# Experts in a fixed order of whole quarters, the embedding's products during the choice of tokens, and the scan's arrays under the first weight buffers

## The chip, the cores and the metric

The kernel runs on one core of a Trainium2 chip. The metric is the device time of one execution in microseconds (us). The kernel before was timed three times: 1959.51, 1963.56 and 1964.66 us, so the median is 1963.56 us. Each time below comes from one profiled execution, and "at 503" means 503 us after the start of its span.

TensorE (PE) runs the matmuls, VectorE (DVE) and ScalarE (ACT) move results out of PSUM and do the small arithmetic, GpSimd (POOL) does some wide additions, and SyncE (SP) issues nearly all DMAs. SP does so strictly in the order of its program: a DMA whose buffer is not yet free holds up all that stand behind it.

## The reference, cut to what matters

Two layers, sequence 512, width 1024, float32. In each layer a mixer (a projection, three groups of sequence operations, among them a gated-delta scan, and an output projection) is followed by the part that the change is about:

```python
def expert_choice_ffn(h, w_router, w_gate, w_up, w_down):
    cap = EC_CAPACITY * S // N_EXPERTS            # 64 tokens for each of 16 experts
    aff = jax.nn.softmax(jnp.einsum('bsd,de->bse', h, w_router), axis=-1)
    gate, idx = lax.top_k(aff.transpose(0, 2, 1), cap)
    xe = jax.vmap(lambda hb, ib: hb[ib])(h, idx)  # gather
    hid = silu(einsum('becd,edf->becf', xe, w_gate)) * einsum('becd,edf->becf', xe, w_up)
    ye = einsum('becf,efd->becd', hid, w_down) * gate[..., None]
    y = zeros((B_ * S, D)).at[flat].add(ye.reshape(-1, D))   # scatter
...
x = x + expert_choice_ffn(rmsnorm(x, g_ffn[i]), ...)
e = rmsnorm(einsum('bsq,qd->bsd', p[i], w_ple[i]), g_ple[i])      # the embedding
x = x + e * sigmoid(rmsnorm(x, g_ple_gate[i]) @ w_ple_gate[i])
```

`w_gate`, `w_up` and `w_down` are 1024x1024 for each of 16 experts: 192 MB of float32 in a layer, and each byte is used once.

## The kernel before

**Pairs and gemms.** The experts run in eight pairs `pi`. An expert has 64 tokens, so two share the 128 output partitions: expert `ei` of a pair writes partitions 64*ei to 64*ei+63. For each pair `gemm` (L1268 to L1279) runs three times: gate into `pGt`, up into `pUp`, down into `pY`. One gemm is four quarters of the inner dimension. A quarter needs one weight tile from each of the two experts, 128x2048 float32 = 1,048,576 bytes, and issues 8 matmuls with `ei` innermost, so two neighbours write different halves of the columns. The trace has two records for each float32 matmul: 16 in a quarter, 64 in a gemm. A layer has 23 such gemms, that is 184 tiles. The 24th, the last pair's down product, is done in column quarters with 16 tiles `wd` of 512 KB (L1387, L1391); the gate of the embedding ends the layer.

**Other work on PE in this stage.** `gather` builds the tokens of two pairs at a time with matmuls `xep` against one-hot matrices (L1206, L1207), with the transposes `otp` and the small products `pgs` (L1220 to L1229). `scatter` multiplies back, `ysc` (L1295, L1296), and DVE adds it to `x` (L1301). Two groups of transposes `htp` (L1349) turn `hid` between up and down. After pair 5 `ple_e` multiplies the embedding, `plep` (L1172), and normalises it (`e`, L1181, L1182).

**The order.** For the first pair the four gate quarters and the first gather are interleaved by hand. All else is left to a scheduler which orders instructions by priority and readiness: a scatter's or gather's matmuls may go into the middle of a quarter.

**The weights.** `etile` (L1250 to L1265) takes the next buffer of the `ring` (L1241): five `wx`, three pairs of buffers of other names (used once), one `gslot`, then twelve `slot`. That is 21 tiles ahead at first. At the first scatter `taken(2)` gives two slots to the new `x`; after pair 5 two more go to `e` and three are moved back in the ring. Tiles stay with the buffer that the ring gives, and SP issues them in the program's order.

**The stages.** In the first layer the mixer goes to about 400 us, the router and the top-k (on DVE, eight rounds) to 446, the experts from 449 to 912 and the tail to about 985. The second layer has the same sequence; its first gate matmul starts 963 us later, at 1412.8. Buffers of the mixer lie where the expert stage's buffers come later; placeholders (`place`, L380 to L383) settle which mixer arrays lie under which.

Of the kernel before, what the change touches and what calls it, by code (L numbers as in the profile page):

```python
# [20 lines left out]
D = 1024  # L21
S = 512
# [95 lines left out]
class K:  # L118
# [938 lines left out]
    def moe(self, l):  # L1057
# [60 lines left out]

        wk = ep.tile([64, S // 2], F32, tag="OT", name="topk", bufs=3)
# [28 lines left out]
        pe.matmul(pr[:, 1], ones, rr_(above[:, 2, None, :]).to_broadcast([128, NT, NE]), start=False, stop=True)  # L1148
        rank = ep.tile([128, NT, NE], F32, name="rank")
# [3 lines left out]
        self.tap("rank", rank)  # L1153
        affr = ep.tile([128, NT, NE, 2], F32, name="affr")
        rsr = ep.tile([128, NT, 2], F32, name="rsr")

        def ple_e():

            self.mark("ple_e")
            gple = self.slot("gple")[:, :D]  # L1160
            self.row(gple, l, "g_ple")
            pTt = self.slot("pT")[:, :2 * S].rearrange("p (k n) -> p k n", k=2)
            nc.scalar.dma_start(pTt, A["pT"][l].rearrange("(k p) t -> p k t", p=128))
            wple = self.wtile(A["w_ple"][l], 1024, nk=2)
            self.ee = [self.slot("e").rearrange("p (t d) -> p t d", t=2) for _ in range(2)]
            es = ep.tile([128, NT, 2], F32, name="es")
            er = ep.tile([128, NT], F32, name="er")
            for t in range(NT):
                for half in range(2):
                    p = self.pb([128, 512], "plep")  # L1170
                    for k in range(2):
                        pe.matmul(p, pTt[:, k, t * 128:(t + 1) * 128], wple[:, k, half * 512:half * 512 + 512],  # L1172
                                  start=(k == 0), stop=(k == 1))
                    ev = e(t)[:, half * 512:half * 512 + 512]
                    act.activation(ev, p, AF.Square, accum_out=es[:, t, half:half + 1])
                    v.tensor_copy(ev, p)
# [7 lines left out]
        e = lambda t: self.ee[t // 2][:, t % 2, :]  # L1184
# [5 lines left out]
        def gather(qd):  # L1190
            self.mark("gather")
            OH = ep.tile([128, NT, 4, CAP], F32, tag="OH", name="OH", bufs=1)
            for t in range(NT):
                v.tensor_tensor(rr_(OH[:, t]), iota[:, None, :].to_broadcast([128, 4, CAP]),  # L1194
                                rank[:, t, 4 * qd:4 * qd + 4, None].to_broadcast([128, 4, CAP]), op=ALU.is_equal)
            OHf = rr_(OH.rearrange("p t e s -> p t (e s)"))
            xe = self.gslot("xe").rearrange("p (k n) -> p k n", k=KD)
            for pi in (0, 1):
                self.xe[2 * qd + pi] = xe[:, :, 128 * pi:128 * pi + 128]
            for kp in range(4):  # L1200
                self.mark("gather")
                for kk in (2 * kp, 2 * kp + 1):
                    p = self.pb([128, 4 * CAP], "xep")
                    ks = every(2, kk)
                    for t in range(NT):
                        pe.matmul(p, rr_(hh[:, t, ks]), OHf[:, t, :], start=(t == 0), stop=False)  # L1206
                        pe.matmul(p, rr_(hl[:, t, ks]), OHf[:, t, :], start=False, stop=(t == NT - 1))  # L1207
                    act.activation(xe[:, kk, :], p, AF.Copy, scale=gE[:, kk:kk + 1])
# [7 lines left out]
            for pi in (2 * qd, 2 * qd + 1):  # L1216
# [4 lines left out]
                OT = ep.tile([128, NT, 128], F32, tag="OT", name="OT", bufs=3)  # L1221
                act.activation(rr_(OT), p.bitcast(F32), AF.Copy)
                pgs = self.pc([128, 6], "pgs")
                for t in range(NT):
                    pe.matmul(pgs[:, 0:4], OHf[:, t, s0:s0 + 128],
                              rr_(affr[:, t, 2 * pi:2 * pi + 2, :].rearrange("p e s -> p (e s)")),
                              start=(t == 0), stop=(t == NT - 1))
                for t in range(NT):
                    pe.matmul(pgs[:, 4:6], OHf[:, t, s0:s0 + 128], rr_(rsr[:, t, :]),  # L1229
                              start=(t == 0), stop=(t == NT - 1))  # L1230

                gsl = ep.tile([128, 4], F32, tag="gsl", name="gsl", bufs=4)
                v.tensor_reduce(gsl[0:64, 0:1], pgs[0:64, 0:2], axis=AX.X, op=ALU.add)
                v.tensor_reduce(gsl[64:128, 0:1], pgs[64:128, 2:4], axis=AX.X, op=ALU.add)
                v.tensor_reduce(gsl[:, 3:4], pgs[:, 4:6], axis=AX.X, op=ALU.add)
                v.tensor_scalar(gsl[:, 1:2], gsl[:, 3:4], 0.5, None, op0=ALU.mult)
                v.tensor_tensor(gsl[:, 2:3], gsl[:, 1:2], gsl[:, 3:4], op=ALU.mult)
                self.OT[pi], self.gsl[pi] = OT, gsl
# [3 lines left out]
                     + ["slot"] * SLOTS)  # L1242
# [24 lines left out]
        def gemm(ws, lhs, pt):  # L1267

            for q in range(4):
                self.mark("experts")  # L1270
                wt = [etile(ws[ei][q * 256:(q + 1) * 256, :]) for ei in range(2)]
                for k in range(2):
                    kk = q * 2 + k
                    for nh in range(2):
                        for ei in range(2):
                            pe.matmul(pt[nh][64 * ei:64 * ei + 64, :], lhs[:, kk, 64 * ei:64 * ei + 64],  # L1276
                                      wt[ei][k][:, nh * 512:nh * 512 + 512],
                                      start=(kk == 0), stop=(kk == KD - 1))
                yield  # L1279

        def run(gen):
            for _ in gen:
                pass

        def scatter(pi, yh, yl):
# [5 lines left out]
            for t in range(NT):  # L1291
                for nh in range(2):
                    ns = slice(nh * 512, nh * 512 + 512)
                    p = self.pb([128, 512], "ysc")
# [5 lines left out]
                    else:  # L1300
                        v.tensor_tensor(xv, p, xv, op=ALU.add)  # L1301

        prev = None
        for pi in range(NE // 2):
            self.mark("experts")
            es_ = [2 * pi, 2 * pi + 1]
            if pi == 0:
                g0 = gather(0)
                piece = self.in_order()
                piece(g0)  # L1310
# [3 lines left out]
            if pi == 0:  # L1314

                for _ in range(4):
                    piece(gate)
                    piece(g0)
                run(g0)
            run(gate)  # L1320
# [3 lines left out]
            for nh in range(2):  # L1324
                sv = sg[:, nh * 512:nh * 512 + 512]
                act.activation(sv, pG[nh], AF.Tanh, scale=gsl[:, 1:2])  # L1326
                v.scalar_tensor_tensor(sv, sv, 1.0, pG[nh], op0=ALU.add, op1=ALU.mult)  # L1327
            pU = [self.pg([128, 512], "pUp") for _ in range(2)]
            run(gemm([A["w_e_up"][l, i] for i in es_], xe, pU))
# [14 lines left out]
            self.mark("experts")  # L1344
            for nh in range(2):
                p = self.pc([128, 4, 128], "htp")
                for k in range(4):
                    kk = nh * 4 + k
                    pe.transpose(p[:, k, :], hid[:, every(2 if pi < NE // 2 - 1 else 4, kk)], self.ident)  # L1349
                act.activation(hidT[:, nh * 4:nh * 4 + 4, :], p, AF.Copy)  # L1350
            if pi == NE // 2 - 1:
                break
            pY = [self.pg([128, 512], "pY") for _ in range(2)]
            run(gemm([A["w_e_down"][l, i] for i in es_], hidT, pY))
# [149 lines left out]
```

## Time and profile before

| | us |
|---|---|
| median of three runs | 1963.56 |
| the profiled execution | 1962.08 |
| its span (first to last instruction) | 1960.3 |
| PE busy in the span | 1809.5 |
| DVE / ACT / POOL busy | 931.7 / 523.9 / 457.4 |
| experts of layer 0 (window 449 to 909): PE busy, DMA share | 456.93, 0.94 |
| experts of layer 1 (window 1412 to 1885): PE busy, DMA share | 467.69, 0.93 |

Busy time is the union of an engine's instructions; a PE that is busy is not PE at its peak, since a matmul that runs alone occupies it as well as two that share it. "DMA share" is the mean busy share of the 16 DMA engines, and GB/s what they moved. In a timeline "x16" is a run of 16 records of one group, its first number the start and its second the time to the end of the last. "[10.25 <-DVE topk L1132]" is idle time just before, and what ended it.

### The profile page before, as it was taken

How to read it: one execution, taken by the hardware profiler on the slowest of the kernel's cores; microseconds unless marked ns; L12 is line 12 of the kernel's file. 1: busy time of each engine (PE TensorE's matmuls, PEld its weight loads, DVE VectorE, ACT ScalarE, POOL GpSimd, SP SyncE). 2: the span in 40 equal slices, each digit the busy share in tenths (PEclk: the TensorE clock that was granted, in tenths of full speed). 3: DMA queues.
4: the chain of work that ended last, by engine and by line, in shares of the span. 5: the costliest groups of instructions: out<-in, count | busy, mean ns of one | idle time of the engine just before them, and what ended most of it. 6: DMA issues, size and time to landing. Idle time of an engine off the chain costs nothing.

```text
span 1960.3 us, 30038 instructions
## 1 busy us (share of the span) xinstructions
PE 1809.5 (92%) x12216; PEld 1140.4 (58%) x12216; DVE 931.7 (48%) x2088; ACT 523.9 (27%) x1213; POOL 457.4 (23%) x402
## 2 busy tenths in 40 slices
PE   6898698979999999999989978899799999999999
PEld 5777665864344444434988767568544344443358
DVE  5879767671112121132778796776511212114126
ACT  4334444331010101102443344552311011011023
POOL 3544313320000003021645452233100000031025
PEclk9998788989999999999998977999799999999999
DMA  5212020187799999899342020202987999998991
GB/s 169 86 33 60 17 85 15 56 329 302 321 423 421 409 421 407 345 412 379 111 134 76 24 74 2 97 2 102 411 321 318 422 421 397 422 394 345 380 328 66
DMA packets 122394, 467.47 MB, mean 238 GB/s; under 512 B 11664, under 2 KB 68496, under 8 KB 75920
## 3 DMA queue, kind: packets, MB, share of 16 engines
q1 hardware_dynamic: 115168, 458.46, 59.5%
q10 hardware_dynamic: 7088, 7.09, 1.2%
q8 instruction: 96, 1.57, 0.3%
q14 instruction: 42, 0.34, 0.1%
HBM read 461.32 MB, written 4.19 MB: 237 GB/s over the span
## 4 chain that ended last, share of the span: by engine, by line
PE 69%; DVE 20%; ACT 3%; issue 3%; POOL 2%; DMA 2%; ACTq 0%; SPq 0%; DVEq 0%; POOLq 0%
PE pGt L1276 14%; PE pUp L1276 11%; PE pY L1276 10%; DVE acc L778 3%; PE xep L1206 2%; PE ysc L1295 2%; DVE rr L944 2%; PE xep L1207 2%; PE pY L1391 2%; PE pV L951 1%; PE op L348 1%; PE ysc L1296 1%; PE pgp L348 1%; PE pgp L350 1%; PE plep L1172 1%
## 5 line engine op out<-in xcount | busy, mean ns | idle before, releaser
L1276 PE MATMUL pGt<-w,xe 128*64 128x512 f32 x592 | 194.8, 607 | 0.0
L340 POOL TENSOR_TENSOR wlo<-w,whi 128x512 fp32r<-128x512 f32 (+5 forms) x66 | 162.1, 2473 | 102.9 <-ACT whi L338 71.9
L1276 PE MATMUL pUp<-w,xe 128*64 128x512 f32 x688 | 178.4, 593 | 0.0
L1343 POOL TENSOR_TENSOR x<-x,hh 128x1024 f32<-128x1024 f32 x8 | 18.8, 2356 | 620.0 <-DMA wx<-in_w_e_up_dram 310.4
L1276 PE MATMUL pY<-w,hidT 128*64 128x512 f32 x608 | 162.5, 596 | 0.2 <-ACT hidT L1350 0.2
L1360 DVE SCALAR_TENSOR_TENSOR yl<-pY,gsl,yh 128x512 fp32r<-128x512 f32 x28 | 21.0, 751 | 203.1 <-ACT yh L1359 201.5
L1301 DVE TENSOR_TENSOR x<-ysc,x 128x512 f32<-128x512 f32 x96 | 62.9, 686 | 110.5 <-PE ysc L1296 110.5
L1276 PEld LDWEIGHTS pUp<-w,xe 128*64 128x64 f32 x688 | 62.9, 137 | 89.5 <-issue 86.3
L1276 PEld LDWEIGHTS pGt<-w,xe 128*64 128x64 f32 x592 | 56.1, 137 | 99.2 <-issue 92.7
L1276 PE MATMUL pGt<-wx,xe 128*64 128x512 f32 x384 | 113.0, 599 | 0.3
L1334 DVE SCALAR_TENSOR_TENSOR hid<-sg,gsl,pUp 128x512 f32<-128x512 f32 x32 | 23.9, 748 | 169.8 <-PE pUp L1276 168.0
L1276 PEld LDWEIGHTS pY<-w,hidT 128*64 128x64 f32 x608 | 55.6, 136 | 76.2 <-issue 73.3
L1276 PE MATMUL pUp<-wx,xe 128*64 128x512 f32 x320 | 99.8, 595 | 0.0
L1276 PE MATMUL pY<-wx,hidT 128*64 128x512 f32 x288 | 86.2, 595 | 0.0
L1327 DVE SCALAR_TENSOR_TENSOR sg<-sg,pGt 128x512 f32<-128x512 f32 x32 | 21.7, 686 | 131.3 <-ACT sg L1326 131.3
L338 ACT ACTIVATE whi<-w 128x512 fp32r<-128x512 f32 (+5 forms) x66 | 68.2, 1058 | 38.5 <-PE op L349 15.8
L1326 ACT ACTIVATE sg<-pGt,gsl 128x512 f32<-128x512 f32 x32 | 21.8, 687 | 196.5 <-PE pGt L1276 194.6
L1350 ACT ACTIVATE hidT<-htp 128x512 f32<-128x512 f32 x32 | 19.0, 597 | 200.4 <-PE htp L1349 200.4
L1206 PE MATMUL xep<-OH,hh 128*128 128x256 f32 x256 | 70.1, 307 | 2.4 <-DVE OH L1194 2.4
L778 DVE SCALAR_TENSOR_TENSOR acc<-raw,pp,acc 128x512 f32<-128x512 f32 x72 | 64.3, 894 | 15.5 <-ACT acc L776 13.0
L348 PE MATMUL pgp<-whi,gTh 128*128 128x256 f32 x256 | 70.9, 281 | 0.0
L350 PE MATMUL pgp<-whi,gTl 128*128 128x256 f32 x256 | 69.8, 282 | 0.3 <-DVE gTl L279 0.3
(404 smaller groups left out, 4277.3 us busy)
## 6 DMA issues: line engine op xcount, KB each, us to landing
w<-in_w_e_up_dram SPq DMA_DIRECT2D x86, 1024.0 KB, 15.4
w<-in_w_e_down_dram SPq DMA_DIRECT2D x76, 1024.0 KB, 12.7
w<-in_w_e_gate_dram SPq DMA_DIRECT2D x74, 1024.0 KB, 15.6
wx<-in_w_e_gate_dram SPq DMA_DIRECT2D x48, 1024.0 KB, 9.9
wx<-in_w_e_up_dram SPq DMA_DIRECT2D x40, 1024.0 KB, 16.7
wx<-in_w_e_down_dram SPq DMA_DIRECT2D x36, 1024.0 KB, 12.0
wd<-in_w_e_down_dram SPq DMA_DIRECT2D x32, 512.0 KB, 8.3
w<-in_w_in_dram SPq DMA_DIRECT2D x14, 1024.0 KB, 5.2
```

The lines of the kernel that those rows point to most:

```text
L338: self.nc.scalar.activation(rr_(hi[:, ks, :]), wk, AF.Copy)
L340: e.tensor_tensor(rr_(lo[:, ks, :]), wk, hi[:, ks, :], op=ALU.subtract)
L348: pe.matmul(p, lh, rh, start=first, stop=False)
L350: pe.matmul(p, ll, rh, start=False, stop=last)
L778: v.scalar_tensor_tensor(acc, raw[:, kk:kk + S], conv[:, b, kk:kk + 1], acc, op0=ALU.mult, op1=ALU.add)
L944: v.tensor_tensor(rr[kl[dr], :], vtok[kl[dr], tl, :], fl(tm[kl[dr]]), op=ALU.subtract)
L1206: pe.matmul(p, rr_(hh[:, t, ks]), OHf[:, t, :], start=(t == 0), stop=False)
L1207: pe.matmul(p, rr_(hl[:, t, ks]), OHf[:, t, :], start=False, stop=(t == NT - 1))
L1276: pe.matmul(pt[nh][64 * ei:64 * ei + 64, :], lhs[:, kk, 64 * ei:64 * ei + 64], wt[ei][k][:, nh * 512:nh * 512 + 512], start=(kk == 0), sto ...
L1295: pe.matmul(p, rr_(OT[:, t, :]), rr_(yh[:, ns]), start=True, stop=False)
L1301: v.tensor_tensor(xv, p, xv, op=ALU.add)
L1391: pe.matmul(pY[64 * ei:64 * ei + 64, :], hidT[:, 4 * half + k, 64 * ei:64 * ei + 64], wt[ei][:, k, :], start=(half + k == 0), stop=(half * ...
```

## The change

1. **Order.** All PE work of the expert stage is now tied into one sequence by `in_order` and `issue_after`. The 8 matmuls of a quarter stand together. Gate: quarter, half a scatter, quarter, half a scatter, quarter, quarter. Up, where a gather is due: half a gather, two quarters, half a gather, two quarters, then `otp` and `pgs`. Then `turn` (the `htp` transposes) and four down quarters. The scatter of a pair thus lies in the next pair's gate gemm.
2. **Banks.** `scatter` alternates between two PSUM pools, `gather` puts two results into one bank, and `pgs` of two pairs share one tile.
3. **Embedding.** `gple`, `pT` and `w_ple` are loaded by SP ahead of the first up tiles, 2 MB in all, where before they were loaded at pair 5 (two of them by ACT). Twelve of 16 `plep` products stand between `pa` and `pth`, that is during the top-k, and four behind `rankp`. ACT copies them into `e`; the squares and the normalisation come after pair 4.
4. **Ring.** Nine slots in place of twelve: two go to `e` and one to `gple` and `pT` from the router on. A tenth joins after pair 4.
5. **Places.** The scan's arrays `KQT`, `kdec0`, `kdec1`, `vtok` and `QKm` join the placeholders, so that they lie under the first weight buffers in place of arrays that are in use longer.

```diff
-                                 ("p1", 512, 3), ("p2", 512, 2)):
+                                 ("p1", 512, 3), ("p2", 512, 2), ("KQT", 3 * NCH * 64, 1), ("kdec0", NT * 384, 1),
+                                 ("kdec1", NT * 384, 1), ("vtok", NT * 384, 1), ("QKm", 48 * 32, 1)):
...
+        nc.sync.dma_start(pTt, A["pT"][l].rearrange("(k p) t -> p k t", p=128))
+        nc.sync.dma_start(gple, A["pr"][l:l + 1, PR["g_ple"][0]:PR["g_ple"][0] + D].to_broadcast([128, D]))
+        wple = self.wtile(A["w_ple"][l], 1024, nk=2)
...
+        def ple_first(ts):
...
+                    p = self.pg([128, 512], "plep")
+                    for k in range(2):
+                        pe.matmul(p, pTt[:, k, t * 128:(t + 1) * 128], wple[:, k, half * 512:half * 512 + 512],
+                                  start=(k == 0), stop=(k == 1))
+                    act.activation(e(t)[:, half * 512:half * 512 + 512], p, AF.Copy)
+        ple_first(range(NT - 1))
...
+        with tc.issue_after(ranked):
+            ple_first((NT - 1,))
...
-                     + ["slot"] * SLOTS)
+                     + ["slot"] * (SLOTS - 3))
...
-                            pe.matmul(pt[nh][64 * ei:64 * ei + 64, :], lhs[:, kk, 64 * ei:64 * ei + 64],
+                            with ExitStack() as st:
+                                if k + nh + ei:
+                                    st.enter_context(tc.issue_after(nc.cur_bb.bb.instructions[-1]))
+                                pe.matmul(pt[nh][64 * ei:64 * ei + 64, :], lhs[:, kk, 64 * ei:64 * ei + 64],
...
-                    p = self.pb([128, 512], "ysc")
+                    p = (self.pc if t % 2 else self.pb)([128, 512], "ysc")
...
+                trace(gate, gate, ga, gate, gate, ga)
+            else:
+                trace(gate, sc, gate, sc, gate, gate)
...
+            if ga is none:
+                trace(up, up, up, up)
+            else:
+                trace(ga, up, up, ga, up, up)
...
-            if prev is not None:
-                scatter(*prev)
-            if pi % 2 and pi < NE // 2 - 1:
-                run(gather(pi // 2 + 1))
+            if ga is not none:
+                piece(ga)
...
-            prev = (pi, yh, yl)
-            if pi == 5:
-                taken(2)
-                taken(3, True)
+            sc = scatter(pi, yh, yl)
+            if pi == 4:
                 ple_e()
+                ring.append("slot")
```

On PE, in the gate gemm of a pair in layer 0 (`pGt`, with the scatter's `ysc`), the program before has:

```order
L1276 MATMUL pGt<-w,xe 64x512 x6
L1295 MATMUL ysc<-yh,OT 128x512
L1296 MATMUL ysc<-yl,OT 128x512
L1276 MATMUL pGt<-w,xe 64x512 x2
L1295 MATMUL ysc<-yh,OT 128x512
L1296 MATMUL ysc<-yl,OT 128x512
L1276 MATMUL pGt<-w,xe 64x512 x6
```

and the changed one, at the same place:

```order
L1301 MATMUL pGt<-w,xe 64x512 x8
L1317 MATMUL ysc<-yh,OT 128x512 x2
L1318 MATMUL ysc<-yl,OT 128x512 x2
L1317 MATMUL ysc<-yh,OT 128x512 x2
L1318 MATMUL ysc<-yl,OT 128x512 x2
L1301 MATMUL pGt<-w,xe 64x512 x8
```

Quarters that were cut into six and two matmuls of the scheduler's choice are whole, with eight scatter matmuls together between them.

On SP, behind the first tiles of layer 0 that go into the ring's first round, the program before has:

```order
L1264 DMA w<-in_w_e_up_dram 128x2048 x7
L1264 DMA w<-in_w_e_down_dram 128x2048 x5
L1264 DMA wz<-in_w_e_up_dram 128x2048
L1264 DMA wx<-in_w_e_down_dram 128x2048 x3
L1264 DMA wx<-in_w_e_gate_dram 128x2048 x2
L1264 DMA w<-in_w_e_gate_dram 128x2048 x6
L1264 DMA w<-in_w_e_up_dram 128x2048 x6
```

and the changed one:

```order
L1124 DMA gple<-in_pT_dram 128x2x512
L1125 DMA gple<-in_pr_dram 128x1024
L297 DMA w<-in_w_ple_dram 128x2x1024
L1286 DMA w<-in_w_e_up_dram 128x2048 x7
L1286 DMA w<-in_w_e_down_dram 128x2048 x2
L1286 DMA wz<-in_w_e_up_dram 128x2048
L1286 DMA wx<-in_w_e_down_dram 128x2048 x5
L1286 DMA w<-in_w_e_down_dram 128x2048
L1286 DMA w<-in_w_e_gate_dram 128x2048 x2
L1286 DMA wx<-in_w_e_gate_dram 128x2048 x2
L1286 DMA wx<-in_w_e_up_dram 128x2048 x3
```

Three fewer down tiles stand ahead of `wz`, the embedding's loads are new ahead of the up tiles, and the buffers that the next tiles take are others.

On PE in layer 0's router (`pa` turns the affinities, `pth` the chosen thresholds), the program before has:

```order
L1110 MATMUL pa<-cst,aff 64x128
L1134 MATMUL pth<-cst,topk 128x32
L1143 MATMUL rankp<-ge,mcr 128x128
...
L1148 MATMUL rankp<-above,mcr 128x64
L1206 MATMUL xep<-OH,hh 128x256
```

and the changed one:

```order
L1111 MATMUL pa<-cst,aff 64x128
L1136 MATMUL plep<-w,gple 128x512 x12
L1158 MATMUL pth<-cst,topk 128x32
L1167 MATMUL rankp<-ge,mcr 128x128
...
L1172 MATMUL rankp<-above,mcr 128x64
L1136 MATMUL plep<-w,gple 128x512 x4
L1221 MATMUL xep<-OH,hh 128x256
```

Twelve `plep` matmuls stand ahead of `pth` and four ahead of the first gather.

## Rows read from the trace of the kernel before

**Rows 1.** The page: busy share of the DMA engines, 40 slices, in tenths.

```profile
DMA  5212020187799999899342020202987999998991
```

**Rows 2.** Windows, both expert stages: length; busy us of each engine; clock; DMA share; GB/s.

```profile
449.00:909.00 460.00, 456.93 (x1997) 197.39 (x1998) 91.81 (x178) 54.08 (x100) 29.37 (x12) 1.00 0.94 385
1412.00:1885.00 473.00, 467.69 (x2026) 200.83 (x2026) 93.77 (x180) 55.16 (x102) 33.36 (x16) 1.00 0.93 380
```

**Rows 3.** The same windows, PE busy with the gemms alone (L1276).

```profile
449.00:909.00 460.00, 360.25 (x1458) 1.00 0.94 385
1412.00:1885.00 473.00, 368.90 (x1472) 1.00 0.93 380
```

**Rows 4.** The first window, PE busy with `plep` alone (L1172).

```profile
449.00:909.00 460.00, 14.16 (x32) 1.00 0.94 385
```

**Rows 5.** PE's timeline: quarters cut by a scatter, then two whole quarters in a row.

```profile
632.41 1.93 PE L1276 MATMUL pGt<-w,xe 128*64 128x512 f32 x4
634.27 0.50 PE L1295 MATMUL ysc<-yh,OT 128*128 128x512 f32 x1
...
635.40 3.65 PE L1276 MATMUL pGt<-w,xe 128*64 128x512 f32 x12
638.98 0.50 PE L1295 MATMUL ysc<-yh,OT 128*128 128x512 f32 x1
...
895.06 3.65 PE L1276 MATMUL pGt<-w,xe 128*64 128x512 f32 x16
898.49 4.03 PE L1276 MATMUL pUp<-w,xe 128*64 128x512 f32 x17
```

**Rows 6.** PE's timeline: a gather's run, `otp` and `pgs` of one pair, a turn.

```profile
642.45 0.39 PE L1206 MATMUL xep<-OH,hh 128*128 128x256 f32 x1
...
644.37 0.28 PE L1207 MATMUL xep<-OH,hl 128*128 128x256 f32 x1
...
606.77 0.54 PE L1220 MATMUL otp<-identr,OH 128*128 128x128 f32 x4
...
608.10 3.65 PE L1276 MATMUL pY<-w,hidT 128*64 128x512 f32 x12
...
912.43 1.61 PE L1349 MATMUL htp<-cst,hid 128*128 128x128 f32 x8
```

**Rows 7.** Windows of 10 us early in layer 0's experts: columns as in rows 2.

```profile
469.00:479.00 10.00, 10.00 (x58) 4.74 (x56) 2.42 (x10) 2.46 (x4) 0.00 (x0) 1.00 0.25 84
...
499.00:509.00 10.00, 10.00 (x48) 3.30 (x46) 1.50 (x2) 1.37 (x2) 0.00 (x0) 1.00 1.01 422
...
519.00:529.00 10.00, 10.00 (x45) 3.22 (x43) 0.00 (x0) 0.00 (x0) 0.00 (x0) 1.00 0.28 116
```

**Rows 8.** What SP waited for, 370 to 930: us in total, times, longest.

```profile
SPq L1264 <- PE pGt L1276: 136.7, 40, 10.9
...
SPq L1264 <- DVE o_sum L1015: 17.8, 1, 17.8
```

**Rows 9.** The weight DMAs of L1264, 448 to 535: from issue to landing.

```profile
DMA to landing us min/median/max: 4.7/8.9/17.3
```

**Rows 10.** Layer 0's router: SP's first expert tiles, then PE's timeline.

```profile
382.27 20.30 SPq L1264 DMA_DIRECT2D wx<-in_w_e_gate_dram  x5
...
442.56 0.31 PE L1134 MATMUL pth<-cst,topk 32*128 32x32 f32 x1 [10.25 <-DVE topk L1132]
...
445.85 0.55 PE L1206 MATMUL xep<-OH,hh 128*128 128x256 f32 x1 [1.19 <-DVE OH L1194]
```

**Rows 11.** Windows of 1 us where the last up tile ends, layer 0 and layer 1.

```profile
903.00:904.00 1.00, 1.00 (x7) 0.39 (x4) 0.00 (x0) 0.00 (x0) 0.00 (x0) 1.00 0.94 381
...
1872.00:1873.00 1.00, 1.00 (x8) 0.46 (x6) 0.00 (x0) 0.00 (x0) 0.00 (x0) 1.00 0.93 377
```

**Rows 12.** Windows of two mixers: PE partly idle, and the clock beside it.

```profile
50.00:60.00 10.00, 8.09 (x46) 7.45 (x45) 7.17 (x12) 4.42 (x8) 4.65 (x2) 1.00 0.35 106
1245.00:1255.00 10.00, 7.54 (x122) 5.80 (x122) 7.14 (x16) 2.78 (x7) 2.51 (x2) 0.83 0.01 2
```

More of the change, by code (lines that the diff above doesn't have):

```diff
@@ L1117, in moe @@
         self.tap("aff", aff)
+        self.ee = [self.slot("e").rearrange("p (t d) -> p t d", t=2) for _ in range(2)]
+        e = lambda t: self.ee[t // 2][:, t % 2, :]
+        gslot_ = self.slot("gple")
+        gple, pTt = gslot_[:, 0:D], gslot_[:, D:2 * D].rearrange("p (k n) -> p k n", k=2)
+        nc.sync.dma_start(pTt, A["pT"][l].rearrange("(k p) t -> p k t", p=128))
+        nc.sync.dma_start(gple, A["pr"][l:l + 1, PR["g_ple"][0]:PR["g_ple"][0] + D].to_broadcast([128, D]))
+        wple = self.wtile(A["w_ple"][l], 1024, nk=2)
+        es = ep.tile([128, NT, 2], F32, name="es")
+        er = ep.tile([128, NT], F32, name="er")
+        def ple_first(ts):
+            self.mark("ple_e")
+            for t in ts:
+                for half in range(2):
+                    p = self.pg([128, 512], "plep")
[4 more added lines that the diff above has]
+        ple_first(range(NT - 1))
+        self.mark("router")
         wk = ep.tile([64, S // 2], F32, tag="OT", name="topk", bufs=3)
@@ L1153, in moe @@
         self.tap("rank", rank)
+        with tc.issue_after(ranked):
+            ple_first((NT - 1,))
+        self.mark("router")
         affr = ep.tile([128, NT, NE, 2], F32, name="affr")
@@ L1159, in ple_e @@
             self.mark("ple_e")
[L1160 to L1167, printed above, removed]
             for t in range(NT):
                 for half in range(2):
[L1170 to L1176, printed above, removed]
+                    junk = ep.tile([128, 512], F32, tag="OT", name="junk", bufs=3)
+                    act.activation(junk, e(t)[:, half * 512:half * 512 + 512], AF.Square,
+                                   accum_out=es[:, t, half:half + 1])
             v.tensor_tensor(er, es[:, :, 0], es[:, :, 1], op=ALU.add)
@@ L1199, in gather @@
                 self.xe[2 * qd + pi] = xe[:, :, 128 * pi:128 * pi + 128]
-            for kp in range(4):
+            for h in range(2):
                 self.mark("gather")
[L1202 to L1208, printed above, removed]
+                for k0 in (4 * h, 4 * h + 2):
+                    p = self.pb([128, 2, 4 * CAP], "xep")
+                    for kk in (k0, k0 + 1):
+                        ks = every(2, kk)
+                        for t in range(NT):
+                            pe.matmul(p[:, kk - k0, :], rr_(hh[:, t, ks]), OHf[:, t, :], start=(t == 0), stop=False)
+                            pe.matmul(p[:, kk - k0, :], rr_(hl[:, t, ks]), OHf[:, t, :], start=False, stop=(t == NT - 1))
+                    for kk in (k0, k0 + 1):
+                        act.activation(xe[:, kk, :], p[:, kk - k0, :], AF.Copy, scale=gE[:, kk:kk + 1])
                 yield
@@ L1215, in gather @@
                 v.tensor_tensor(rr_(rsr[:, :, 1]), rs, rsr[:, :, 0], op=ALU.subtract)
-            for pi in (2 * qd, 2 * qd + 1):
+            both = (2 * qd, 2 * qd + 1)
+            for pi in both:
                 s0 = 128 * (pi % 2)
@@ L1220, in gather @@
                     pe.transpose(p[:, t, :], OHf[:, t, s0:s0 + 128], identr)
-                OT = ep.tile([128, NT, 128], F32, tag="OT", name="OT", bufs=3)
-                act.activation(rr_(OT), p.bitcast(F32), AF.Copy)
-                pgs = self.pc([128, 6], "pgs")
+                self.OT[pi] = ep.tile([128, NT, 128], F32, tag="OT", name="OT", bufs=3)
+                act.activation(rr_(self.OT[pi]), p.bitcast(F32), AF.Copy)
+            pgs = self.pb([128, 2, 6], "pgs")
+            for pi in both:
+                s0 = 128 * (pi % 2)
                 for t in range(NT):
-                    pe.matmul(pgs[:, 0:4], OHf[:, t, s0:s0 + 128],
+                    pe.matmul(pgs[:, pi % 2, 0:4], OHf[:, t, s0:s0 + 128],
                               rr_(affr[:, t, 2 * pi:2 * pi + 2, :].rearrange("p e s -> p (e s)")),
@@ L1275, in gemm @@
                         for ei in range(2):
[L1276 to L1278 removed]
+                            with ExitStack() as st:
+                                if k + nh + ei:
+                                    st.enter_context(tc.issue_after(nc.cur_bb.bb.instructions[-1]))
+                                pe.matmul(pt[nh][64 * ei:64 * ei + 64, :], lhs[:, kk, 64 * ei:64 * ei + 64],
+                                          wt[ei][k][:, nh * 512:nh * 512 + 512],
+                                          start=(kk == 0), stop=(kk == KD - 1))
                 yield
[L1281 to L1283 removed]
         def scatter(pi, yh, yl):
@@ L1301, in scatter, with turn, trace @@
                         v.tensor_tensor(xv, p, xv, op=ALU.add)
-        prev = None
+                if t % 2:
+                    yield
+        def turn(hid, hidT, by):
+            self.mark("experts")
+            for nh in range(2):
+                p = self.pc([128, 4, 128], "htp")
+                for k in range(4):
+                    pe.transpose(p[:, k, :], hid[:, every(by, nh * 4 + k)], self.ident)
+                act.activation(hidT[:, nh * 4:nh * 4 + 4, :], p, AF.Copy)
+            yield
+        piece = self.in_order()
+        def trace(*gens):
+            for gen in gens:
+                piece(gen)
+        last, none = NE // 2 - 1, iter(())
+        sc = none
         for pi in range(NE // 2):
@@ L1327, in moe @@
                 v.scalar_tensor_tensor(sv, sv, 1.0, pG[nh], op0=ALU.add, op1=ALU.mult)
+            ga = gather(pi // 2 + 1) if pi % 2 and pi < last else none
             pU = [self.pg([128, 512], "pUp") for _ in range(2)]
-            run(gemm([A["w_e_up"][l, i] for i in es_], xe, pU))
+            up = gemm([A["w_e_up"][l, i] for i in es_], xe, pU)
+            if ga is none:
+                trace(up, up, up, up)
+            else:
+                trace(ga, up, up, ga, up, up)
             hid = ep.tile([128, 1024], F32, tag="hid", name="hid", bufs=1)
@@ L1343, in moe @@
                         pool_e.tensor_tensor(self.x(t), self.x(t), part[:, t, :], op=ALU.add)
[L1344 to L1351, printed above, removed]
+            piece(turn(hid, hidT, 2 if pi < last else 4))
+            if pi == last:
                 break
             pY = [self.pg([128, 512], "pY") for _ in range(2)]
-            run(gemm([A["w_e_down"][l, i] for i in es_], hidT, pY))
+            down = gemm([A["w_e_down"][l, i] for i in es_], hidT, pY)
+            trace(down, down, down, down)
             yh = ep.tile([128, 1024], F32, tag="yh", name="yh", bufs=1)
```

25 lines of the change are left out of this document (11 added, 14 removed).

## The prediction

> **What bounds the kernel now.** First the DMA line of the page [rows 1]: the experts of the two layers (slices 9 to 18 and 29 to 38) have DMA engines near full and slices of 7 and 8 between. The windows of the two stages [rows 2] put this in numbers: PE is busy 456.93 of 460 us and 467.69 of 473, DMA 0.94 and 0.93 at 385 and 380 GB/s. Where nothing stops it DMA runs at 422 [rows 7]; I use 421. So it loses 460 x (1 - 385/421) = 39 us in layer 0 and 473 x (1 - 380/421) = 46 in layer 1. Both engines look full, and the question is which of them is full for a reason. The timeline answers it for PE [rows 5]. Two whole quarters follow each other by 898.49 - 895.06 = 3.43 us, since matmuls on different halves of the columns run together. A quarter that the scheduler cut by a scatter took 634.27 - 632.41 = 1.86 for its first four records and 638.98 - 635.40 = 3.58 for the other twelve: 5.44. All 64 records of a gemm at the paired pace need 4 x 3.43 = 13.73, which is 0.2145 each. The gemms' busy time by itself [rows 3] is 360.25 for 1458 records, 312.7 at that pace, and 368.90 for 1472, 315.8. PE therefore spends 47 and 53 us per layer on matmuls that run alone. Then DMA: its holes are 0.25 at 469 to 479 and 0.28 at 519 to 529 [rows 7], and SP's longest account is waiting for `pGt`, 136.7 us in 40 waits [rows 8]. DMA stands because PE hasn't yet given back the buffer for which SP waits. So PE is the bound early in each stage and now and then later, DMA is the bound elsewhere, and the gain from a faster PE ends where DMA is full.
>
> **DMA's floor.** A tile of 1,048,576 bytes takes 2.49 us at 421 GB/s, 184 of them 458. After the change PE needs about 457 - 47 - 14 = 396 us in the stage (14.16 is `plep` [rows 4], which leaves it). For six gemms, that is two pairs, it is 6 x 13.73, a gather of 2 x 3.9 (16 matmuls from 642.45 to 644.37 are 0.12 us apart, 32 in a half), `otp` and `pgs` of 2 x 1.33, two turns of 1.6 plus a little, 1.75, [rows 6], and two scatters of 16 matmuls, 0.24 each from the records at 634 [rows 5]: 82.4 + 7.8 + 2.7 + 3.5 + 7.8 = 104. The 48 tiles of six gemms need 119.5. PE becomes the faster of the two; the time is that of DMA and of what still stops it.
>
> **What still stops it.** I walk through layer 0, at the full clock.
> - Router. `pth` waits 10.25 us for the top-k and starts at 442.56 [rows 10]. The twelve `plep` matmuls, 14.16/16 = 0.885 each [rows 4], take 10.6 from 432.3 and lie in that idle time; `pth` then starts at about 442.9. If the hole weren't there, they would cost the 10.6. The four others, 3.5 us, partly hide in the 1.19 before the first gather; that starts at 448.3 in place of 445.85 [rows 10]. Its first half of 32 matmuls goes to 452.2. Before it ran at half pace (0.21 us apart, clock 0.50 in the idle stretch); with PE busy before it I take 0.12. The second half follows later, so the first up quarter starts within 1 us of before: the router costs about 0, and between -2 and +4.
> - The gate quarters end at 455.6, 459.1, 466.4 (the second half of the gather lies between) and 469.8, the up quarters at 475.7, 479.1, 482.5 and 486.0, the down quarters at 491.1, 494.6, 498.0 and 501.5.
> - DMA has 18 tiles ahead in place of 21. Tiles 19 to 23 are the five `wx` of the first down, which take the buffers of gate tiles: four run from 456.5 to 466.5, the fifth from 467.3 to 469.9. I take 0.9 us from a release to the restart; a lone DMA lands after 4.7 [rows 9], of which 2.49 is its own transfer. Tile 24 needs a slot that the first up quarter frees: 476.6 to 479.1. Tiles 25 and 26 run from 480 to 485. Tile 27 is again a `wx` and waits until the second down quarter is done, at 494.6, though slots for the tiles behind it on SP are free by then. It restarts at 495.5. In all DMA stands 3.5 + 0.8 + 6.8 + 0.9 + 10.5 = 22.5 us, and from there I find no further wait: in each pair the next request's buffer is freed before DMA comes to it.
> - So 26 of 184 tiles are in at 495.5, and 158 x 2.49 = 393.4 later, at 888.9, the last up tile. Before, the windows where the rate falls from 421 to the tail's pace of about 355 put it at 903.4 and 1872.3 [rows 11], the latter being 909.2 in layer 0's clock (963.1 us between the two first gate matmuls). The gain is 14.5 and 20.3 us. The ledger agrees: 39 - 22.5 - 3 fewer tiles ahead (7.5) + 2 MB of embedding loads that leave the stage (5) = 14, and 46 - 30 + 5 = 21.
>
> The tail's `wd` tiles follow the last up tile at once and DMA is full there too, so the end moves with it.
>
> **The other parts.** *Places:* SP's first gate tile waited 17.8 us for `o_sum` [rows 8] and was done with five at 402 [rows 10]; now it waits for the scan's products only, which end near 382. The buffers that can be filled ahead are the same 18, and the last of them are freed only by the router, so the earlier start is worth 0, at most 2. It also brings the 2 MB of the embedding before 432: eight gate tiles and 2 MB from 382 on are 25 us. *Banks:* a half scatter's 8 matmuls take 1.9 us and DVE's four adds about 2.6; at most 0.8 per half, under DMA. *New wait:* a scatter stands in the fixed order and needs `yl`, while the quarter ahead of it lasts 3.43 us; work behind it on PE can't pass. With PE 15 us ahead per six gemms, a wait of 1 or 2 us costs nothing. *Embedding's squares* move from pair 5 to pair 4: 0. All in all -35 us.
>
> 1962.1 - 34.8 = 1927.3; the profiled run lies 1.5 below the median of 1963.56, and I let that stand.
>
> **Rivals.**
> - *More of the holes go.* If SP reaches the next tile without waiting for down's second quarter, or the buffers come free earlier, only the first ring's few us remain. All 39 + 46 less 2.5 a layer would give 1882; half of the 45 us of holes that I leave gives 1905. Against it: 18 tiles ahead can't cover a first pair that takes PE 50 us and DMA 60. 12%, 1895 to 1914.
> - *The ring stalls again.* There are nine slots in place of twelve, and SP's order is rigid: one late `wx` in each pair holds up all behind it. A stall of 2 us in each of the seven pairs left takes 28 of the 35 us back: 1955. For it: SP's waits for `pGt` now [rows 8]. Against it: PE's lead grows from pair to pair. 14%, 1940 to 1957.
> - *Nothing is gained*: the quarters whole in the program don't run paired on the chip, because a quarter that waits for the second expert's tile runs its matmuls alone. PE stays at 457 - 14, and 14 us of that is the only gain, about the price of the smaller ring: 1962. Against it: whole quarters at 895.06 ran paired. 7%.
> - *Slower: the clock.* A PE that waits for DMA in each quarter may drop to 1.2 GHz. Rows for it: 7.54 us busy of 10 at a mean clock of 0.83; against it 8.09 at 1.00 [rows 12], and 1.00 in both stages now [rows 2]. PE's 104 us per six gemms outlast DMA's 119.5 from a mean clock of 0.87 down. At 0.75 they are 139, 19.5 too many for each six of the 14 gemms behind the middle of the third pair: 45 per layer, 90 less the 35 gained: 2017. But a PE at half the clock is busy all the time, and a busy PE shows 1.00 [rows 2], so it should climb back. 7%.
>
> On this the Trainium skill ("TensorE: Matmul & The Clock Gate", section "Loop structure matters more than you think") says that a loop which waits for DMA ahead of its matmuls runs cold, while back-to-back matmuls stay warm. It speaks against a change that makes PE wait on DMA: by it alone the last rival's 2017 would be the time. The rows above agree only in part, as PE with 8.09 of 10 kept its clock.
>
> **How the numbers follow.** 60% for the forecast, 1927, its own range 1914 to 1940; the rivals 12, 14, 7 and 7%. The range 1905 to 1950 leaves out half of the first rival, a third of the second, and the last two, about 2 in 10 or a little more. About 0.3%, 6 us, is what a measurement of this kernel can tell from no change: faster means under 1957.7. That is the forecast, the first rival and nearly all of the second: 0.85; same 0.08 (the third rival and the end of the second), slower 0.07.
>
> **What would show it.** Gemms at 313 to 316 us per layer in place of 360 and 369. DMA holes before about 496 and none after it up to the last up tile, near 889 in layer 0, with the stage at 400 GB/s or more. `plep` in 432 to 443, at clock 1.00. PE's idle time in the later quarters ended by weight DMAs, 60 us or so per layer. SP's waits on `pGt` and `pUp` in the later pairs without a hole in DMA. I am wrong if DMA shows holes after 500, if the clock in 600 to 880 is under 0.9, or if `pth` starts after 445.

## The result, and the profile after

The changed kernel takes 1931.69 us (median of four runs, 1928.21 to 1935.14); beside it the kernel before had 1961.53 (1954.32 to 1964.66). The ratio is 0.9869, 95% interval 0.9848 to 0.9890. The profiled execution took 1928.21 us with a span of 1926.4, which is 33.9 less than before; the prediction's sum was 34.8. That is a comparison of two single executions, and the one of the change is the fastest of its four. By the ratio the gain is 26 us, between 22 and 30.

First the page: PE's busy time, and the DMA engines' busy share in 40 slices, to be set beside [rows 1].

```profile
PE 1744.0 (91%) x12216; PEld 1101.6 (57%) x12216; DVE 920.0 (48%) x2072; ACT 529.9 (28%) x1229; POOL 460.7 (24%) x402
...
DMA  5212020187899999999342020204769999999981
```

Behind the first slices of each expert stage it is all nines, where before there were slices of 7 and 8 up to the end. The windows of layer 0's experts behind the start (columns as in [rows 2]):

```profile
500.00:560.00 60.00, 54.25 (x270) 25.68 (x268) 10.38 (x27) 6.91 (x14) 0.00 (x0) 0.94 1.01 422
560.00:880.00 320.00, 299.96 (x1384) 123.51 (x1380) 67.20 (x124) 37.05 (x70) 29.13 (x12) 0.98 1.01 421
```

DMA moves 421 to 422 GB/s without a break for 380 us, and PE is idle for 26 of them. SP still waits there for buffers that PE holds (`pUp` 27.8 us, `pY` 25.4 and `pGt` 23.6 between 520 and 880), without a hole in DMA. PE's timeline at the end of the stage shows who waits for whom:

```profile
880.95 3.65 PE L1301 MATMUL pUp<-wx,xe 128*64 128x512 f32 x16 [1.31 <-DMA wx<-in_w_e_up_dram]
885.92 3.65 PE L1301 MATMUL pUp<-wx,xe 128*64 128x512 f32 x16 [1.32 <-DMA wx<-in_w_e_up_dram]
```

Each of these rows starts at the same place of a quarter: behind its first two records, where PE waits for the second expert's tile. They lie 885.92 - 880.95 = 4.97 us apart. That is two tiles of 2.49, the floor that the prediction worked out, and no longer the 3.43 of PE. The last up tile ends where the rate falls, in these windows of 1 us (before: [rows 11]):

```profile
887.00:888.00 1.00, 1.00 (x7) 0.29 (x4) 0.00 (x0) 0.00 (x0) 0.00 (x0) 1.00 0.97 376
...
1834.00:1835.00 1.00, 1.00 (x8) 0.35 (x5) 0.00 (x0) 0.00 (x0) 0.00 (x0) 1.00 1.00 386
```

With the first gate matmul of each layer the span falls into five stretches. All rows below come from the two profiled executions; the ends are interpolated in the 1 us windows.

| stretch | before, us | after, us | difference |
|---|---|---|---|
| start to first gate matmul, layer 0 | 449.7 | 448.4 | -1.3 |
| to the last up tile, layer 0 | 453.7 | 438.9 | -14.8 |
| to the first gate matmul, layer 1 | 509.4 | 509.1 | -0.3 |
| to the last up tile, layer 1 | 459.5 | 438.1 | -21.4 |
| to the end | 87.9 | 91.9 | +4.0 |

In these two executions the gain lies in the two expert stages, and nowhere else. The kernel before has this one profile, so how far its stages vary isn't known; those of the change lie within 2 us of each other in two executions.

### The profile page after: what moved, and what is told of

Same layout as the page of the kernel before. It is cut to its first block, busy times and chain, and to the rows that moved or that the text cites. A ratio compares the mean times of both kernels' runs of the same rounds, so it can differ in the third digit from the quotient of the medians.

```text
span 1926.4 us, 30012 instructions
## 1 busy us (share of the span) xinstructions
PE 1744.0 (91%) x12216; PEld 1101.6 (57%) x12216; DVE 920.0 (48%) x2072; ACT 529.9 (28%) x1229; POOL 460.7 (24%) x402
## 4 chain that ended last, share of the span: by engine, by line
PE 53%; DMA 21%; DVE 18%; ACT 3%; issue 3%; POOL 2%; SPq 0%; DVEq 0%; ACTq 0%; POOLq 0%
PE pGt L1301 8%; DMA w<-in_w_e_up_dram 7%; PE pUp L1301 7%; PE pY L1301 6%; DMA w<-in_w_e_gate_dram 5%; DMA wx<-in_w_e_down_dram 4%; DVE acc L779 3%; DMA wx<-in_w_e_gate_dram 2%; DVE rr L945 2%; PE plep L1136 2%; PE xep L1221 2%; PE op L348 2%; PE pgp L350 1%; PE pgp L348 1%; PE pV L952 1%
## 5 line engine op out<-in xcount | busy, mean ns | idle before, releaser
L1301 PE MATMUL pGt<-w,xe 128*64 128x512 f32 x704 | 171.8, 609 | 12.7 <-DMA w<-in_w_e_gate_dram 12.7
L1301 PE MATMUL pY<-wx,hidT 128*64 128x512 f32 x528 | 143.2, 594 | 11.2 <-DMA wx<-in_w_e_down_dram 11.2
L1198 POOL TENSOR_TENSOR e<-e,gple 128x1024 f32<-128x1024 f32 x8 | 21.0, 2650 | 516.7 <-DVE e L1197 516.7
L1301 PE MATMUL pUp<-wx,xe 128*64 128x512 f32 x400 | 114.8, 596 | 6.4 <-DMA wx<-in_w_e_up_dram 6.4
L1301 PE MATMUL pY<-w,hidT 128*64 128x512 f32 x368 | 114.9, 634 | 1.5 <-ACT hidT L1333 0.8
L337 POOL TENSOR_TENSOR w<-w,pp 128x512 f32<-128x512 f32 x32 | 32.3, 1041 | 304.4 <-DMA w<-in_w_ple_gate_dram 170.9
L1301 PEld LDWEIGHTS pY<-wx,hidT 128*64 128x64 f32 x528 | 45.1, 137 | 101.0 <-issue 80.4
L1323 DVE TENSOR_TENSOR x<-ysc,x 128x512 f32<-128x512 f32 x96 | 59.7, 684 | 78.8 <-PE ysc L1318 78.8
L338 ACT ACTIVATE whi<-w 128x512 fp32r<-128x512 f32 (+5 forms) x66 | 68.5, 1058 | 37.6 <-PE op L349 15.8
L1301 PE MATMUL pGt<-wx,xe 128*64 128x512 f32 x272 | 71.4, 608 | 7.7 <-DMA wx<-in_w_e_gate_dram 7.7
L1394 ACT ACTIVATE yh<-pY,gsl 128x512 fp32r<-128x512 f32 x28 | 19.2, 687 | 202.0 <-PE pY L1301 202.0
L1301 PEld LDWEIGHTS pUp<-wx,xe 128*64 128x64 f32 x400 | 35.3, 137 | 67.4 <-issue 51.2
```

The source lines that it names most:

```text
L337: self.nc.gpsimd.tensor_tensor(wk, wk, gain[:, ks, None].to_broadcast([128, step, cols]), op=ALU.mult)
L338: self.nc.scalar.activation(rr_(hi[:, ks, :]), wk, AF.Copy)
```

## The experiments

Each run is given as a ratio to the kernel before, timed on the same chip. Beside it stands the length of the two expert stages in its profiled execution (first gate matmul to last up tile, layer 0 and layer 1; good to about 1 us, since the end is interpolated). The second is the sharper measure, since the rest of the span varies: the first gate matmul lay between 442.7 and 453.7 us in executions whose mixers are nearly the same program.

| run | ratio, 95% interval | stages, us |
|---|---|---|
| before | 1 | 453.7, 459.5 |
| the change | 0.9869 (0.9848 to 0.9890) | 438.9, 438.1 |
| the change, on another chip job | 0.9880 (0.9863 to 0.9897) | 440.4, 439.0 |
| free order | 0.9891 (0.9868 to 0.9914) | 440.6, 441.6 |
| old places | 0.9888 (0.9868 to 0.9907) | 439.3, 438.3 |
| products in the stage | 0.9870 (0.9848 to 0.9891) | 438.8, 437.6 |
| before, with tied quarters | 0.9906 (0.9885 to 0.9926) | 441.8, 446.3 |
| free order and products in the stage | 1.0022 (1.0006 to 1.0037) | 456.2, 454.9 |
| 3.8 us more PE work per pair | 0.9904 (0.9887 to 0.9920) | 438.8, 438.2 |
| 12.8 us more PE work per pair | 1.0240 (1.0222 to 1.0257) | 458.7, 459.1 |
| tiles in the order of use | 0.9810 (0.9786 to 0.9835) | 431.9, 431.5 |
| the same, on another chip job | 0.9800 (0.9773 to 0.9827) | 431.1, 431.1 |

The repeat of the change, against which the runs of its job are set:

> The changed kernel once more, on the chip of the three runs beside it, so that they can be set against it: 0.985 to 0.989 of the kernel before.

1931.82 us, 0.9880: as expected.

**The order taken away.** From the second pair on nothing is tied:

```diff
-                            with ExitStack() as st:
-                                if k + nh + ei:
-                                    st.enter_context(tc.issue_after(nc.cur_bb.bb.instructions[-1]))
-                                pe.matmul(pt[nh][64 * ei:64 * ei + 64, :], lhs[:, kk, 64 * ei:64 * ei + 64],
+                            pe.matmul(pt[nh][64 * ei:64 * ei + 64, :], lhs[:, kk, 64 * ei:64 * ei + 64],
...
+                piece = lambda gen: next(gen, None)
```

> The change with its fixed order taken away from the second pair on: quarters, scatters and gathers are again the scheduler's to place, all else is kept. My theory (the gain is PE giving back buffers sooner because matmuls run in pairs; the rest of the time is DMA): the scheduler cuts only some gate quarters here, so PE's gemms take perhaps 10 to 20 us more per layer than in the changed kernel, most of it under DMA; 1936 to 1948, that is 4 to 16 us over the changed kernel's 1932. Rival (the gain comes from the embedding's products and the ring, not from the order): 1932 within 3. Rival (the order is all of the gain): 1955 or more.

1935.40 us, just under what I expected, and by the ratios 4 more than the change, with intervals that overlap. The reason that I gave doesn't hold, though. PE busy with the gemms, in the windows 440 to 912 and 1380 to 1885, first in the change, then with the free order, then a window of the stage with the free order:

```profile
440.00:912.00 472.00, 341.18 (x1472) 0.98 0.97 394
1380.00:1885.00 505.00, 342.40 (x1472) 0.98 0.94 381
```

```profile
440.00:912.00 472.00, 364.55 (x1472) 1.00 0.97 394
1380.00:1885.00 505.00, 366.13 (x1472) 1.00 0.94 382
...
560.00:870.00 310.00, 308.49 (x1337) 136.42 (x1335) 65.91 (x122) 35.55 (x68) 29.12 (x12) 1.00 1.01 420
```

The gemms are busy as long as before, 364.55 and 366.13 against 363.25 (in the same window of the kernel before) and 368.90 [rows 3]. Counted in PE's records, the scheduler cuts 17 of a layer's 92 quarters, where it cut 24 and 25. These 17 hold 34 us over the paired pace, where the 24 and 25 held 43 and 47. Still DMA is full, 420 GB/s, beside a PE that is busy 308.49 of 310 us. So the matmuls that run alone weren't by themselves what emptied DMA's queue.

**The matmuls of a quarter tied, in the kernel before:**

```diff
+                            with ExitStack() as st:
+                                if k + nh + ei:
+                                    st.enter_context(tc.issue_after(nc.cur_bb.bb.instructions[-1]))
+                                pe.matmul(pt[nh][64 * ei:64 * ei + 64, :], lhs[:, kk, 64 * ei:64 * ei + 64],
```

> The kernel before with one thing added: the 8 matmuls of a quarter are tied in a row; ring, embedding, places, banks and the order of gathers and scatters stay as before. My theory: PE sheds most of its 47 and 53 us of unpaired time, three more tiles are ahead than in the changed kernel, and 2 MB of embedding loads stay in the stage; DMA's holes come down to about 25 us per layer, and the time is 1925 to 1942, most of the change's gain. Rival (the gain needs the embedding's products out of the stage, or the new rotation of buffers): 1948 to 1962.

1938.34 us, 0.9906: 7 us from the change and 18 from the kernel before, in the range of my theory. This part alone brings most of the gain as well. It does less than I wrote, however, since the edit leaves a quarter's first matmul free. In 24 of 92 quarters other work still stands behind it, here a gather:

```profile
627.79 1.07 PE L1279 MATMUL pGt<-w,xe 128*64 128x512 f32 x2
628.80 0.39 PE L1206 MATMUL xep<-OH,hh 128*128 128x256 f32 x1
...
630.93 3.65 PE L1279 MATMUL pGt<-w,xe 128*64 128x512 f32 x14
```

The gemms' busy time is 347.54 and 348.91 us: PE sheds 16 and 20 us per layer, and not most of its 47 and 53. The last 7 us of the change may come from any of its other parts; no run separates them.

**The products back in the stage:**

```diff
-        ple_first(range(NT - 1))
...
-        with tc.issue_after(ranked):
-            ple_first((NT - 1,))
...
         def ple_e():
+            ple_first(range(NT))
```

> The changed kernel, but its 16 products of the embedding go back into the expert stage (after pair 4); their loads and buffers stay where the change put them. My theory: 14 us of PE work per layer come back into a stage where PE has some 60 us to spare, so they cost nothing there; the router starts the gathers 2 us sooner at the half clock, one down tile's buffer comes free a little later or sooner; 1929 to 1942. Rival (PE is still the bound in the stage, the gain is the 14 us per layer that left it): 1956 to 1962.

1931.85 us, 0.9870: nothing is lost. With the fixed order, 14 us of PE work per layer cost nothing.

**Both taken away.** Two parts whose removal costs 4 and 0 us, and of which one brings 18 in the kernel before, can't be added up. The next run has neither, while ring, banks and places are those of the change.

> The changed kernel with both taken away: the order is free from the second pair on (as in the run with the free order) and the embedding's products are back in the expert stage (as in the run with the products there). Ring, banks and places stay as changed. The two runs lost 4 and 0 us by themselves. Theory A (PE before needed just as long as DMA, and either relief, the paired matmuls or the 14 us of products, is enough to put DMA in front): with both gone PE is the bound again and DMA shows holes after pair 4; 1948 to 1960. Theory B (the new rotation of the ring and the two buffers taken early did it, whatever PE does): 1934 to 1944.

1961.82 us, 1.0022: all the gain is gone, and 4 us more. It is theory A, with a time 2 us above its range. Moving the products out alone (the run with the free order) takes 26 us off this time, close to their 14 us per layer. Windows of this kernel around and behind the products, which PE runs from 699 to 742, and the stage as a whole:

```profile
730.00:740.00 10.00, 10.00 (x27) 3.29 (x26) 1.50 (x2) 2.64 (x6) 0.00 (x0) 1.00 0.56 204
...
780.00:790.00 10.00, 10.00 (x46) 4.93 (x44) 0.00 (x0) 1.00 (x3) 0.49 (x1) 1.00 0.63 245
790.00:800.00 10.00, 10.00 (x45) 4.84 (x45) 1.44 (x3) 2.21 (x4) 0.00 (x0) 1.00 0.62 218
...
560.00:870.00 310.00, 309.29 (x1314) 135.03 (x1312) 59.73 (x112) 38.36 (x74) 29.11 (x12) 1.00 0.97 398
```

PE is busy all the time, as with the free order alone, but its work is 14 us longer, and in these three windows DMA moves about half of what it could. SP's longest waits there, 725 to 805, are for buffers that PE holds:

```profile
SPq L1283 <- PE pGt L1295: 28.7, 7, 8.2
SPq L1283 <- PE pUp L1295: 27.8, 6, 8.5
```

PE's and DMA's needs were almost equal before, 457 and 458 us in the prediction's sum. Paired matmuls or the absence of 14 us: either brings PE down to DMA's pace, and the second of them finds nothing more to gain. By themselves ring, banks and places bring nothing, since this run has them too.

**How much PE has to spare.** From the third pair on n matmuls whose result nobody reads stand ahead of each turn; with n = 16 they take 3.77 us, with n = 56 12.84.

```diff
+            if pi > 1:
+                p = self.pc([128, 512], "extra")
+                for i in range(n):
+                    pe.matmul(p, identr, rr_(hh[:, 0, 0:512]), start=(i == 0), stop=(i == n - 1))
```

> The changed kernel with 16 matmuls of 128x512 that nobody reads ahead of each turn from the third pair on: about 3.8 us of PE work more per pair, 23 per layer. My theory: PE needs 52 us and DMA 59.7 for a pair, so 3.8 us disappear in PE's idle time; within 3 us of the changed kernel. Rival (PE at its dipping clock is the bound): 20 to 46 us over it.

> The same with 56 matmuls, about 13.4 us per pair, 80 per layer. My theory: beyond the 7.6 us that a pair has to spare each further us counts, 5.8 x 6 = 35 per layer less what is left of the tiles ahead and of the tail's start: 45 to 70 us over the changed kernel. Were PE the bound already, it would be 160; were the spare larger than I think, nothing.

The first took 1936.46 us, 4.6 over the change in the same job. That is more than the 3 that I allowed, but it isn't in the stages: 438.8 and 438.2 us, the same as without the matmuls. Ten of the twelve groups stand there, so 38 us of PE work cost nothing. The last pair's group stands behind the last up quarter, in the tail:

```profile
892.70 3.93 PE L1332 MATMUL extra<-hh,identr 128*128 128x512 f32 x16
```

From that quarter to the end of the embedding's gate, layer 0 took 87.4 us, against 82.0 in the repeat of the change; layer 1 took 87.4 against 87.3. So the matmuls may cost something in the tail of layer 0; one execution of each doesn't settle it. The second run took 2003.9, 72 over the change, a little above the expected 45 to 70. From the first gate matmul to the last up quarter on PE it took 468.9 us in both layers, against 442.3 and 441.1. Of the 5 x 12.84 = 64.2 us that stand there 37.6 and 36.4 were absorbed, 7.5 and 7.3 per pair; the prediction's 59.7 - 52.1 is 7.6. The rest of the 72 us lies in the tails (8) and in the mixers (10), where executions differ. In its window DMA has holes again and PE none:

```profile
560.00:870.00 310.00, 309.17 (x1481) 151.61 (x1478) 59.16 (x112) 32.76 (x64) 29.22 (x12) 0.99 0.96 395
```

**The places:**

```diff
-                                 ("p1", 512, 3), ("p2", 512, 2), ("KQT", 3 * NCH * 64, 1), ("kdec0", NT * 384, 1),
-                                 ("kdec1", NT * 384, 1), ("vtok", NT * 384, 1), ("QKm", 48 * 32, 1)):
+                                 ("p1", 512, 3), ("p2", 512, 2)):
```

> The changed kernel without the scan's five arrays among the placeholders: SP's first gate tile waits for o_sum again and starts about 18 us later. My theory: the tiles that can be filled ahead are limited by buffers, not by the start, so the time stays within 3 us of the changed kernel, and the first gathers start at the same time unless the embedding's loads now land after 428 and hold up the products ahead of pth, which would cost up to 8 us per layer. Rival (the earlier start is part of the gain): 6 to 15 us over the changed kernel.

1934.82 us, 3 over the change, with intervals that overlap and the same stages (439.3, 438.3). The earlier first tile brings nothing that can be measured here.

**SP's order.** The walk ahead of the result left 10.5 us at one place: SP stands at a `wx` tile that waits for the second down quarter of the first pair, with tiles behind it whose slots are free. Tying the tiles from the second pair on in the order of their use puts four gate tiles ahead of it:

```diff
+            with ExitStack() as st:
+                if line:
+                    st.enter_context(tc.issue_after(line[-1]))
+                nc.sync.dma_start(tv, src)
+            if started:
+                line.append(nc.cur_bb.bb.instructions[-1])
...
+            if pi == 1:
+                started.append(1)
```

> The changed kernel with SP's tiles of the pairs from the second on tied to the order in which PE uses them. Only one place moves: four gate tiles of the second pair, whose slots are free at 486 to 492, stand ahead of the two gate and three up tiles in wx buffers, which wait until the second down quarter of the first pair is done. My theory (the time left over DMA's floor is the holes of the first pair): the hole at 485 to 495 shrinks by some 8 us in each layer, DMA is full after it, and the time falls by 14 to 20 us: 1912 to 1918. Rival (DMA isn't the bound any more after the change, but PE with its dips of the clock): 1930 within 4.

> The changed kernel with SP's tiles in the order of use, once more, to narrow its interval: 0.979 to 0.984 of the kernel before.

1919.49 and 1917.41 us in two jobs, ratios 0.9810 and 0.9800: some 13 us below the change, and the fastest version here. The gain is a little under the 14 to 20 expected. The stages are 7 to 9 us shorter each, which is most of the hole. The window at 480 in the change, then in this version:

```profile
480.00:490.00 10.00, 9.78 (x48) 3.75 (x46) 1.50 (x2) 1.19 (x2) 0.00 (x0) 1.00 0.28 117
```

```profile
480.00:490.00 10.00, 9.75 (x50) 3.75 (x46) 1.50 (x2) 1.19 (x2) 0.00 (x0) 1.00 0.87 332
```

The order that the program had given SP also let PE wait: it stood 4.82 us for a gate tile that SP issued behind five others needed later.

```profile
508.84 1.77 PE L1301 MATMUL pGt<-w,xe 128*64 128x512 f32 x2 [4.82 <-DMA w<-in_w_e_gate_dram]
```

That wait cost nothing by itself, as DMA was full then; the hole ahead of it did.

## Why the prediction was right, and where its steps were not

- **DMA's floor and the walk: right.** Each stage was to gain 14.5 and 20.3 us and gained 14.8 and 21.4 in the profiled pair. The holes up to 500 were to be 22.5 us; from the rates of the windows between 450 and 500 (325, 256, 199, 117 and 286 GB/s against 421) they are 2.3 + 3.9 + 5.3 + 7.2 + 3.2 = 21.9, and none follows. The run in SP's order confirms the largest of them by removing most of it.
- **The size: right in the profiled pair, too large in the timed runs.** The 33.9 of the two profiled executions is near the 34.8, but the timed gain is 22 to 30 us. So the close agreement is in part luck: the sum started from the one profile of the kernel before, 1962.08, while its medians in the later runs were 1957 to 1958.
- **What filled DMA: half right.** I named the 47 and 53 us of unpaired matmuls as what PE must shed. The sum beside it said that PE needed 457 us and DMA 458, and I didn't draw the conclusion: at such a tie any 14 us will do. The run with the free order keeps 34 us per layer of the unpaired time and most of the gain.
- **The rival "nothing is gained": a wrong price.** It said that without pairing, with only the 14 us of products gone, the time would be 1962, since the smaller ring eats them. The run with the free order comes near that case, with all but 8 to 13 us of the unpaired time kept, and took 1935. The term that was mis-sized is the ring's price, put at the whole 14 us per layer. The run with neither relief has the new ring, and lies 4 us above the kernel before; taking the products out of the stage then brings 26.
- **Router: right in sum by luck, wrong in its parts.** The first gate matmul came at 448.4, not 452.2. It lies 20.7 us behind the second `pa` matmul, where the walk had 20.3 and the kernel before 17.9, so the router itself costs 2.9 us; but that matmul came 4.2 earlier than before, of which 2.1 were there at the end of the scan already, and other executions of the same mixer differ by as much. The twelve products filled the wait as foreseen, 1.2 us longer than reckoned, beside a clock of 0.89 (428 to 440) in place of 1.00:

```profile
427.90 11.80 PE L1136 MATMUL plep<-w,gple 128*128 128x512 f32 x24
439.64 0.24 PE L1158 MATMUL pth<-cst,topk 32*128 32x32 f32 x1
```

- **Gemms at 313 to 316 us: wrong,** they are 341 and 342, and none is cut. Of the 26 us over 92 x 3.43 in layer 0, 17 lie in the 22 quarters with a wait ahead of them or inside; in 19 of these PE waits inside, since the second expert's tile comes later than the first. Behind the first two records at 508.84, for example, 14 records take 5.90 us; at the paired pace they take 3.0:

```profile
511.33 5.90 PE L1301 MATMUL pGt<-w,xe 128*64 128x512 f32 x14 [0.73 <-DMA w<-in_w_e_gate_dram]
```

With more PE work, in the run of 3.8 us, fewer quarters wait inside (8 in place of 19 in layer 0), and the gemms' busy time falls to 332 and 334. For the same reason PE's idle time is 26 us from 500 to 880, and not the 60 foretold: part of the time to spare counts as busy.
- **The clock: it fell, and in the stages it cost nothing.** Two windows of the change:

```profile
510.00:520.00 10.00, 9.27 (x27) 3.37 (x28) 2.02 (x4) 0.00 (x0) 0.00 (x0) 0.71 1.02 424
...
780.00:790.00 10.00, 7.29 (x31) 3.89 (x33) 1.24 (x10) 2.28 (x4) 0.00 (x0) 0.66 1.02 421
```

The Trainium skill ("TensorE: Matmul & The Clock Gate", section "Loop structure matters more than you think") says that a long wait for DMA between matmuls leaves PE cold. The trace agrees for the first window: PE had just waited 4.82 us for a tile, and parts of the next matmuls ran at the 1.2 GHz level. In the second window the wait was one of 2.71 us for the copies of `OT`, and not for DMA. Waits of 1.3 us, as at 880.95 and 885.92, left the clock at 1.00. The mean over 560 to 880 is 0.98, far from the 0.87 at which it would have decided; the 0.75 of that rival's 2017 had no row behind it.
- **The tail: a new wait that I hadn't seen.** "The end moves with it" is true in layer 0. In layer 1 the end took 4.0 us longer, of which this wait is 2.8. What PE waited for there, 1864 to 1895 in the change and 1900 to 1930 before:

```profile
PE pgp L350 <- DVE gTl L279: 3.1, 2, 2.9
```

```profile
PE pgp L350 <- DVE gTl L279: 0.3, 1, 0.3
```

PE comes to the gate of the embedding sooner than DVE has `gTl` ready. The repeat (2.9) and the version in SP's order (2.4) wait there too. From 1880 to 1890 the clock is 0.83. Why DVE is later relative to PE there than in layer 0 wasn't tried.

## What to carry to other kernels

When two engines need the same time in a stage, several small reliefs on one of them are alternatives and don't add up: test each alone and none at all before you credit one. Work out the floor of the other engine first; here it gave the length of the stages within about 1 us in the profiled pair, without any need to know which edit would bring PE down to it. Then look at the order of the DMA queue itself, where one request that waits for a late buffer closes the way for those behind it: putting the requests in the order of use gained another 13 us.

## What the runs showed of the hardware that was not expected

The weight stream keeps 420 GB/s beside a PE that is busy 308.49 of 310 us and beside one that isn't; PE's work didn't slow it here. PE's busy time grows when PE waits more: 341 us for the gemms of layer 0 in the change, 332 with 3.8 us of other work per pair in the same stage time. Here, then, a busy time can't be compared between a kernel that waits and one that doesn't.
